# Block-diagonal operands of a block inverse: 48 small copies on one engine, or 16 wide copies on two

## The chip, the cores and the metric

The kernel runs on one core of a Trainium2 chip. The metric is the device time of one execution, in microseconds (us).

## The reference

One step of a diffusion backbone with one trunk layer, on 128 context tokens and 512 latent tokens of width 1024. A modulated RMSNorm is followed by one wide input projection. Its columns feed a bidirectional gated DeltaNet with 8 heads of size 128, a convolution branch and two merge gates; then come an output projection with a gated residual and a gated feed-forward part.

The change concerns the DeltaNet. For each head, direction and chunk of tokens a lower triangular system with unit diagonal is solved:

```
a_mat = where(strict, (k*beta) @ k.T * decay, 0) + I
sol   = triangular_solve(a_mat, [v*beta, k*beta*exp(gc)])
```

The kernel takes chunks of 128 tokens (five of them), and forms the inverse of the 128x128 matrix itself.

## The kernel before

The 640 tokens are the columns of all wide tiles. Heads are worked on in four pairs; a pair has 2 directions x 2 heads x 5 chunks = 20 matrices, ten for each direction. Every pair goes through the same stages, each a generator whose steps are interleaved by weights (`W_PREP`, `W_SUBST`, `W_BUILD`, `W_INV`, `W_SCAN`) with the projections of the later heads, the gates and the convolution (`mains`). What is written there is a program order with priorities; the order of each engine's queue is then settled at compile time from estimated costs. On the chip every engine works its queue in that order.

- `pair_prep` builds the 20 matrices `Bt` (VectorE and ScalarE, with a select on GpSimd, line 590), then inverts the 32x32 diagonal blocks of all of them at once by substitution: line 598 (ScalarE) and line 599 (VectorE) gather the blocks into `Cc`, line 601 transposes, line 604 masks, lines 610 and 612 are 30 steps of two small operations, on VectorE for three pairs and on GpSimd for the last (`SUBST_V`). Lines 616 and 617 write `T1` and `T2`: 32 partitions for each of four diagonal blocks, and for each partition 32 x 32 values, with the matrix number running innermost.
- `pair_inverse` spreads these blocks into block-diagonal 128x128 operands: `XA` from `T1` for the first direction and `T2` for the second, `XB` the other way round. This is line 631. A source element lies 128 bytes from the next. The operands are five tiles each of four matrices; four of the tiles hold four matrices of one direction, the fifth the last two of both. `XB` is cleared once at the start (line 447); `XA` in each pair (line 625), since its tiles are reused later for a product.
- `invert(k)` runs five lanes in turn, step by step: the off-diagonal part `ct` (GpSimd, line 654), products with `XA` (lines 665, 666), with `XB` (line 668), the square written back over `XA` (line 669), the rest (lines 671 to 680). All matmuls of these are in line 660.
- `pair_scan` and `pair_out` carry the state over the chunks and finish the heads.

Wherever a weight is loaded, ScalarE writes its high part (line 109) and VectorE or GpSimd its low part (line 110), before TensorE's projections in line 147. VectorE also runs the depthwise convolution of the other branch, one step for each tap (lines 847 to 854), with two inputs in SBUF. Line 873 evicts a projection through ScalarE, line 875 goes on with it on VectorE.

Of the kernel before, what the change touches and what calls it, by code (L numbers as in the profile page):

```python
# [11 lines left out]
F16 = mybir.dt.float16  # L12
BF16 = mybir.dt.bfloat16
I32 = mybir.dt.int32
AF = mybir.ActivationFunctionType
ALU = mybir.AluOpType
# [3 lines left out]
P = 128  # L20
# [25 lines left out]
W_BUILD = 2.0  # L46
# [12 lines left out]
def hybrid_step(ctx, tc, I, O):  # L59
    nc = tc.nc  # L60
    es = ctx.enter_context
    V, S_, G, PE = nc.vector, nc.scalar, nc.gpsimd, nc.tensor
# [11 lines left out]
    s1p = s1_open.enter_context(tc.tile_pool(name="s1", bufs=1))  # L74
# [10 lines left out]
    def const(name, shape, dt=F32, pool=None):  # L85
        return (pool or sb).tile(list(shape), dt, name=name, bufs=1)
# [18 lines left out]
    def bc(ap, shape):  # L105
        return ap.to_broadcast(shape)
# [66 lines left out]
    for k, (nm, n) in enumerate((("c_ctx", 8), ("c", 8), ("norm1", 8), ("norm2", 8))):  # L173
        src = I[nm] if nm == "c_ctx" else I[nm][0]
# [5 lines left out]
    ident = const("ident", [P, P])  # L180
# [51 lines left out]
    for n in range(2):  # L232
        for i in range(NCH):
            junk = T_("C", "junk")
            S_.activation(junk[:, :512], xs[n][:, i, :], AF.Square, accum_out=ss[:, i, n:n + 1])
            pt = sm_ps()
# [6 lines left out]
    for c0, cn in GRP:  # L243
        pt = g3(sm_ps(), 4)
# [19 lines left out]
    for pr in range(4):  # L264
# [7 lines left out]
        for kk in range(NK):  # L272
            for g in range(4):
                j, k = g // 2, g % 2
                PE.matmul(pa[32 * g:32 * g + 32, :P], sc[:, kk, 14:46], ws[j][:, kk, 128 * k:128 * k + 128],
                          start=(kk == 0), stop=(kk == NK - 1), tile_position=(0, 32 * g))
        br = T_("dd", "br")[:, :P]
        V.tensor_copy(br, pa[:, :P])
        pt = sm_ps()
        PE.transpose(pt[:, :P], br, ident)  # L280
        for k in range(2):
# [5 lines left out]
            for r, (c0, n) in enumerate(SPANS):  # L287
                v, hi, lo = (t[kt // 4][:, kt % 4, c0:c0 + n] for t in (xT, hh, hl))
                b = modB[:, kt, r:r + 1]
# [151 lines left out]

    y32s = [const("y32", [P, 512], pool=s1p)]
    L16 = [const(f"L16{i}", [P, 4, P], F16, s1p) for i in range(9)]
    XA = [const(f"XA{i}", [P, 4, P], F16, s1p) for i in range(5)]
    XB = [const(f"XB{i}", [P, 4, P], F16, s1p) for i in range(5)]
    for t in XB:
        G.memset(t, 0.0)

    def proj_in(col, after=None):
        w = pre.pop(col, None) or load_w(cols_of(w_in, col), after=after)  # L450
# [169 lines left out]

    def pair_inverse(R):
        Bt, Bn, T1, T2 = R.Bt, R.Bn, R.T1, R.T2
        groups = [((0, 4, k % 2, 4 * (k // 2)),) for k in range(4)] + [((0, 2, 0, 8), (2, 2, 1, 8))]
        for k, parts in enumerate(groups):
            G.memset(XA[k], 0.0)
            for o, cnt, d, n0 in parts:
                n0 += 10 * d
                for b in range(4):
                    r = slice(32 * b, 32 * b + 32)
                    for dst, src in ((XA[k], T1 if d == 0 else T2), (XB[k], T2 if d == 0 else T1)):  # L630
                        S_.activation(dst[r, o:o + cnt, 32 * b:32 * b + 32],  # L631
                                      src[r, :, n0:n0 + cnt].rearrange("p o n -> p n o"), AF.Identity)
            yield W_BUILD
        Bd = Bt[:, :2560].rearrange("p (d n i) -> p d n i", d=2, n=10)

        def invert(k):
            xa, xb = XA[k], XB[k]
            ct, a, atr = L16[3 * k:3 * k + 3]
            zt, a2, yt, rr = ct, xa, atr, a
            if k < 4:  # L640
                d, n0 = k % 2, 4 * (k // 2)
                B4, off = Bd[:, d, n0:n0 + 4, :], off16[:, d:d + 1, :]
                shape = [P, 4, P]

                def v(t):
                    return t
            else:
                B4, off = Bd[:, :, 8:10, :], off16.unsqueeze(2)
                shape = [P, 2, 2, P]

                def v(t):
                    return t.rearrange("p (a b) i -> p a b i", a=2)
            blocks = [B4[:, j, :] if k < 4 else B4[:, j // 2, j % 2, :] for j in range(4)]
            G.tensor_tensor(out=v(ct), in0=B4, in1=bc(off, shape), op=ALU.mult)
            yield

            def mm4(lhs, rhs):
                pt = g3(sm_ps(), 4)
                for j in range(4):
                    PE.matmul(pt[:, j, :], lhs[j], rhs[:, j, :], start=True, stop=True)  # L660
                return pt

            def l4(t):
                return [t[:, j, :] for j in range(4)]
            S_.activation(a, mm4(l4(ct), xa), AF.Identity)
            S_.activation(atr, mm4(l4(xa), ct), AF.Identity)
            yield
            V.tensor_tensor(out=zt, in0=mm4(l4(a), xb), in1=xb, op=ALU.add)
            S_.activation(a2, mm4(l4(atr), a), AF.Identity)
            yield  # L670
            V.tensor_tensor(out=yt, in0=mm4(l4(a2), zt), in1=zt, op=ALU.add)
            yield
            ptr = g3(sm_ps(F16), 4)
            for j in range(4):
                PE.transpose(ptr[:, j, :], yt[:, j, :], ident16)
            y32 = g3(y32s[k % 2], 4)
            S_.activation(y32, ptr, AF.Identity)
            V.tensor_tensor(out=rr, in0=mm4(blocks, y32), in1=bc(ident.unsqueeze(1), [P, 4, P]), op=ALU.add)
            yield
            V.tensor_tensor(out=B4, in0=v(mm4(l4(rr), yt)), in1=v(yt), op=ALU.add)  # L680
            yield

        lanes = [invert(k) for k in range(5)]
        while lanes:
            for ln in list(lanes):
                if next(ln, 0) == 0:
                    lanes.remove(ln)
                else:
                    yield W_INV
        R.Y1 = Bn  # L690
# [596 lines left out]
```

## Time and profile before

| | |
|---|---|
| median of 3 runs | 1381.05 us (1378.54 to 1384.46) |
| the profiled execution | 1383.22 us, its span 1381.2 us |
| TensorE busy | 1291.9 us, 94% of the span |
| VectorE busy | 839.1 us, 61% |
| ScalarE busy | 542.0 us, 39% |
| GpSimd busy | 306.8 us, 22% |
| mean granted clock of TensorE | 0.973 of full speed |

In the profile PE is TensorE, DVE is VectorE, ACT is ScalarE, POOL is GpSimd; L631 is line 631 of the kernel. Matmuls are pipelined and their ends are modelled, so a busy TensorE is not one at its peak. A row of a timeline merges neighbouring instructions of one kind (x6 for six), gives their start and length, and in brackets how long the engine stood idle before them and what it was then released by. A row of stretches gives from:to and length, then the busy time (and instructions) of PE, of its weight loads, of DVE, ACT and POOL, or of the one engine concerned, and last TensorE's granted clock, the busy share of the DMA engines and GB/s.

### The profile page before, as it was taken

The page shows a single profiled execution, that of the slowest core. Times are in us where ns is not written, and L with a number is a line of the kernel's source. Part 1 is how long each engine was busy: PE and PEld are TensorE (multiplying, and loading weights), DVE is VectorE, ACT ScalarE, POOL GpSimd, SP SyncE. Part 2 cuts the span into 40 slices and gives each one's busy share as a digit, 9 for nine tenths or more (in the row PEclk, how much of TensorE's full clock was granted, in tenths as well). Part 3 has the DMA queues.
Part 4 walks back from the last instruction along what each step waited for, and adds up shares of the span by engine and source line. Part 5 has one row for each costly group of instructions (what it writes and reads, how often), then busy time and mean ns, then how long its engine had stood idle before and what let it go on. Part 6 is the DMA issues. An engine that isn't in the chain of part 4 may idle for free.

```text
span 1381.2 us, 23408 instructions
## 1 busy us (share of the span) xinstructions
PE 1291.9 (94%) x9180; PEld 1213.3 (88%) x9180; DVE 839.1 (61%) x1603; ACT 542.0 (39%) x1240; POOL 306.8 (22%) x354
## 2 busy tenths in 40 slices
PE   4998996978999998988999989999999999999997
PEld 4998895977998998888989988889998999989996
DVE  5788985978667899596577774731223321233236
ACT  3337647263454555526454133332221222212223
POOL 2103310200010310291010025433310333003314
PEclk8999998999999999998999999999999999999999
DMA  9523442343343543323346884122222222222222
GB/s 289 140 64 113 125 149 80 112 136 100 113 119 99 160 118 94 103 66 94 118 150 212 250 284 148 46 74 77 77 77 76 77 77 77 76 76 69 71 77 91
DMA packets 180334, 157.31 MB, mean 114 GB/s; under 512 B 9072, under 2 KB 151809, under 8 KB 180225
## 3 DMA queue, kind: packets, MB, share of 16 engines
q1 hardware_dynamic: 180225, 155.83, 36.5%
q8 instruction: 72, 1.18, 0.4%
q14 instruction: 37, 0.30, 0.1%
HBM read 131.80 MB, written 24.00 MB: 113 GB/s over the span
## 4 chain that ended last, share of the span: by engine, by line
PE 68%; DVE 13%; ACT 6%; DMA 5%; issue 4%; POOL 1%; SPq 1%; POOLq 0%; DVEq 0%; ACTq 0%
PE mm L147 46%; PE sm L1115 9%; PE mm L1115 4%; DMA wr<-in_w_in 3%; ACT XA L631 2%; ACT XB L631 2%; PE sm L660 2%; DVE wl L110 1%; DVE uacc L847 1%; DVE acc L484 1%; PE sm L736 1%; ACT wh L109 1%; PE sm L495 1%; PE mm L469 1%; DMA og<-ogd 1%
## 5 line engine op out<-in xcount | busy, mean ns | idle before, releaser
L109 ACT ACTIVATE wh<-wr 128x1024 fp32r<-128x1024 f32 (+1 forms) x154 | 152.6, 992 | 497.5 <-PE mm L147 209.3
L147 PE MATMUL mm<-hh,wh 128*128 128x256 f32 (+1 forms) x896 | 219.7, 320 | 11.6 <-ACT wh L109 7.8
L147 PE MATMUL mm<-hl,wh 128*128 128x256 f32 (+1 forms) x896 | 218.0, 317 | 0.0
L147 PE MATMUL mm<-hh,wl 128*128 128x256 f32 (+1 forms) x896 | 216.4, 317 | 0.0
L110 POOL TENSOR_TENSOR wl<-wr,wh 128x1024 fp32r<-128x1024 f32 (+1 forms) x59 | 133.2, 2260 | 345.9 <-ACT wh L109 337.5
L110 DVE TENSOR_TENSOR wl<-wr,wh 128x1024 fp32r<-128x1024 f32 (+1 forms) x95 | 110.0, 1158 | 126.0 <-ACT wh L109 114.9
L147 PEld LDWEIGHTS mm<-hh,wh 128*128 128x128 f32 x896 | 163.5, 192 | 17.7 <-ACT wh L109 8.3
L147 PE MATMUL mm<-h2h,wh 128*128 128x256 f32 (+1 forms) x704 | 165.0, 312 | 1.5 <-ACT h2h L109 1.5
L147 PEld LDWEIGHTS mm<-hl,wh 128*128 128x128 f32 x896 | 166.3, 192 | 0.0
L147 PE MATMUL mm<-h2l,wh 128*128 128x256 f32 (+1 forms) x704 | 164.9, 312 | 0.9 <-POOL h2l L110 0.9
L147 PEld LDWEIGHTS mm<-hh,wl 128*128 128x128 f32 x896 | 164.6, 191 | 0.5 <-DVE wl L110 0.2
L147 PE MATMUL mm<-h2h,wl 128*128 128x256 f32 (+1 forms) x704 | 164.3, 311 | 0.3 <-DVE wl L110 0.3
L1253 DVE TENSOR_TENSOR ft<-ft,mm 128x384 f32<-128x384 f32 (+1 forms) x44 | 19.7, 484 | 198.8 <-PE mm L147 198.6
L147 PEld LDWEIGHTS mm<-h2l,wh 128*128 128x128 f32 x704 | 130.5, 191 | 1.1 <-POOL h2l L110 1.1
L147 PEld LDWEIGHTS mm<-h2h,wh 128*128 128x128 f32 x704 | 129.2, 190 | 1.9 <-ACT h2h L109 1.7
L147 PEld LDWEIGHTS mm<-h2h,wl 128*128 128x128 f32 x704 | 130.0, 190 | 0.6 <-DVE wl L110 0.6
L484 DVE SCALAR_TENSOR_TENSOR acc<-ci,colA,acc 128x642 f32<-128x642 f32 x96 | 85.9, 895 | 7.8 <-ACT acc L482 7.2
L1115 PE MATMUL sm<-wh,fl 128*128 128x512 f32 x152 | 60.0, 395 | 0.0
L1115 PE MATMUL sm<-wh,fh 128*128 128x512 f32 x152 | 59.9, 394 | 0.0
L1115 PE MATMUL sm<-wl,fh 128*128 128x512 f32 x152 | 59.7, 392 | 0.0
L110 DVE TENSOR_TENSOR fl<-ft,fh 128x640 fp32r<-128x640 f32 x22 | 47.7, 2167 | 15.5 <-ACT fh L109 15.5
L847 DVE SCALAR_TENSOR_TENSOR uacc<-u,colB,uacc 128x113 f32<-128x113 f32 (+14 forms) x120 | 47.8, 399 | 0.9
(341 smaller groups left out, 2431.7 us busy)
## 6 DMA issues: line engine op xcount, KB each, us to landing
wr<-in_w_in SPq DMA_DIRECT2D x56, 512.0 KB
wr<-in_w_gu SPq DMA_DIRECT2D x44, 512.0 KB
wr<-in_w_ada SPq DMA_DIRECT2D x32, 512.0 KB
wr<-in_w_down SPq DMA_DIRECT2D x22, 512.0 KB
wada<-in_w_ada SPq DMA_DIRECT2D x8, 1024.0 KB
atd<-et SPq DMA_DIRECT2D x40, 128.0 KB
aux<-atd SPq DMA_DIRECT2D x40, 128.0 KB
tgd<-tgt SPq DMA_DIRECT2D x16, 320.0 KB
```

What stands on the lines that cost most here:

```text
L109: S_.activation(hi, x, AF.Identity)
L110: return (lo_eng or V).tensor_tensor(out=lo, in0=x, in1=hi.bitcast(F32), op=ALU.subtract)
L147: PE.matmul(out, a[:, kt, :], x, start=(kt == 0 and j == 0), stop=(kt == nk - 1 and j == 2))
L469: PE.matmul(pa[32 * g:32 * g + 32, :], sc[:, kt, o:o + 32], w[:, c:c + P], start=(bb == 0), stop=(bb == 1), tile_position=(0, 32 * g))
L484: V.scalar_tensor_tensor(out=acc[:, :n], in0=ci[:, k:k + n], scalar=vA[:, k, ct:ct + 1], in1=acc[:, :n], op0=ALU.mult, op1=ALU.add)
L495: PE.transpose(pt[:, c, :], src(c0 + c), ident)
L631: S_.activation(dst[r, o:o + cnt, 32 * b:32 * b + 32], src[r, :, n0:n0 + cnt].rearrange("p o n -> p n o"), AF.Identity)
L660: PE.matmul(pt[:, j, :], lhs[j], rhs[:, j, :], start=True, stop=True)
L736: PE.matmul(pv[:, d, j, :], Y1[:, d, j, ck[d], :], rhs, start=True, stop=True)
L847: V.scalar_tensor_tensor(out=acc[:, a0:128 - a1], in0=u[:, a0 + dl:128 - a1 + dl], scalar=tap(k, t4), in1=acc[:, a0:128 - a1], op0=ALU.mul ...
L1115: PE.matmul(acc[i], a[kt // 4][:, kt % 4, c], b[:, k2, :], start=(kt == 0 and j == 0), stop=(kt == nk - 1 and j == 2))
L1253: V.tensor_tensor(out=d, in0=d, in1=s, op=ALU.mult)
```

## The change

The ten tiles become two, `XA` and `XB`, each with all 20 matrices of a pair. One copy now moves the same diagonal block of all ten matrices of a direction: 8 copies on ScalarE for `XA`, 8 on GpSimd for `XB`, in place of 48 on ScalarE. `XA` is cleared by one write in place of five, `XB` too. The lanes read and write slices of the two tiles; the operations on them keep their engines and sizes. The fill yields twice with 2.5 times the weight instead of five times.

```diff
--- before.py
+++ after.py
@@ -441,10 +441,8 @@
 
     y32s = [const("y32", [P, 512], pool=s1p)]
     L16 = [const(f"L16{i}", [P, 4, P], F16, s1p) for i in range(9)]
-    XA = [const(f"XA{i}", [P, 4, P], F16, s1p) for i in range(5)]
-    XB = [const(f"XB{i}", [P, 4, P], F16, s1p) for i in range(5)]
-    for t in XB:
-        G.memset(t, 0.0)
+    XA, XB = (const(nm, [P, 2, 10, P], F16, s1p) for nm in ("XA", "XB"))
+    G.memset(XB.rearrange("p d n i -> p (d n i)"), 0.0)
 
     def proj_in(col, after=None):
         w = pre.pop(col, None) or load_w(cols_of(w_in, col), after=after)
@@ -620,64 +618,63 @@
 
     def pair_inverse(R):
         Bt, Bn, T1, T2 = R.Bt, R.Bn, R.T1, R.T2
-        groups = [((0, 4, k % 2, 4 * (k // 2)),) for k in range(4)] + [((0, 2, 0, 8), (2, 2, 1, 8))]
-        for k, parts in enumerate(groups):
-            G.memset(XA[k], 0.0)
-            for o, cnt, d, n0 in parts:
-                n0 += 10 * d
-                for b in range(4):
-                    r = slice(32 * b, 32 * b + 32)
-                    for dst, src in ((XA[k], T1 if d == 0 else T2), (XB[k], T2 if d == 0 else T1)):
-                        S_.activation(dst[r, o:o + cnt, 32 * b:32 * b + 32],
-                                      src[r, :, n0:n0 + cnt].rearrange("p o n -> p n o"), AF.Identity)
-            yield W_BUILD
+        G.memset(XA.rearrange("p d n i -> p (d n i)"), 0.0)
+        for d in range(2):
+            for b in range(4):
+                r = slice(32 * b, 32 * b + 32)
+                S_.activation(XA[r, d, :, 32 * b:32 * b + 32],
+                              (T1, T2)[d][r, :, 10 * d:10 * d + 10].rearrange("p o n -> p n o"), AF.Identity)
+                G.tensor_copy(XB[r, d, :, 32 * b:32 * b + 32],
+                              (T2, T1)[d][r, :, 10 * d:10 * d + 10].rearrange("p o n -> p n o"))
+            yield 2.5 * W_BUILD
         Bd = Bt[:, :2560].rearrange("p (d n i) -> p d n i", d=2, n=10)
 
         def invert(k):
-            xa, xb = XA[k], XB[k]
             ct, a, atr = L16[3 * k:3 * k + 3]
-            zt, a2, yt, rr = ct, xa, atr, a
+            zt, yt, rr = ct, atr, a
             if k < 4:
                 d, n0 = k % 2, 4 * (k // 2)
                 B4, off = Bd[:, d, n0:n0 + 4, :], off16[:, d:d + 1, :]
+                xa, xb = XA[:, d, n0:n0 + 4, :], XB[:, d, n0:n0 + 4, :]
                 shape = [P, 4, P]
 
                 def v(t):
                     return t
             else:
                 B4, off = Bd[:, :, 8:10, :], off16.unsqueeze(2)
+                xa, xb = XA[:, :, 8:10, :], XB[:, :, 8:10, :]
                 shape = [P, 2, 2, P]
 
                 def v(t):
                     return t.rearrange("p (a b) i -> p a b i", a=2)
-            blocks = [B4[:, j, :] if k < 4 else B4[:, j // 2, j % 2, :] for j in range(4)]
+
+            def l4(t):
+                return [t[:, j, :] if len(t.shape) == 3 else t[:, j // 2, j % 2, :] for j in range(4)]
+            a2 = xa
             G.tensor_tensor(out=v(ct), in0=B4, in1=bc(off, shape), op=ALU.mult)
             yield
 
             def mm4(lhs, rhs):
                 pt = g3(sm_ps(), 4)
                 for j in range(4):
-                    PE.matmul(pt[:, j, :], lhs[j], rhs[:, j, :], start=True, stop=True)
+                    PE.matmul(pt[:, j, :], lhs[j], rhs[j], start=True, stop=True)
                 return pt
-
-            def l4(t):
-                return [t[:, j, :] for j in range(4)]
-            S_.activation(a, mm4(l4(ct), xa), AF.Identity)
-            S_.activation(atr, mm4(l4(xa), ct), AF.Identity)
+            S_.activation(a, mm4(l4(ct), l4(xa)), AF.Identity)
+            S_.activation(atr, mm4(l4(xa), l4(ct)), AF.Identity)
             yield
-            V.tensor_tensor(out=zt, in0=mm4(l4(a), xb), in1=xb, op=ALU.add)
-            S_.activation(a2, mm4(l4(atr), a), AF.Identity)
+            V.tensor_tensor(out=v(zt), in0=v(mm4(l4(a), l4(xb))), in1=xb, op=ALU.add)
+            S_.activation(a2, v(mm4(l4(atr), l4(a))), AF.Identity)
             yield
-            V.tensor_tensor(out=yt, in0=mm4(l4(a2), zt), in1=zt, op=ALU.add)
+            V.tensor_tensor(out=yt, in0=mm4(l4(a2), l4(zt)), in1=zt, op=ALU.add)
             yield
             ptr = g3(sm_ps(F16), 4)
             for j in range(4):
                 PE.transpose(ptr[:, j, :], yt[:, j, :], ident16)
             y32 = g3(y32s[k % 2], 4)
             S_.activation(y32, ptr, AF.Identity)
-            V.tensor_tensor(out=rr, in0=mm4(blocks, y32), in1=bc(ident.unsqueeze(1), [P, 4, P]), op=ALU.add)
+            V.tensor_tensor(out=rr, in0=mm4(l4(B4), l4(y32)), in1=bc(ident.unsqueeze(1), [P, 4, P]), op=ALU.add)
             yield
-            V.tensor_tensor(out=B4, in0=v(mm4(l4(rr), yt)), in1=v(yt), op=ALU.add)
+            V.tensor_tensor(out=B4, in0=v(mm4(l4(rr), l4(yt))), in1=v(yt), op=ALU.add)
             yield
 
         lanes = [invert(k) for k in range(5)]
```

## Rows read from the trace of the kernel before

**Rows 1.** Stretches of the span: from:to, length, busy us of each engine.

```profile
120.00:200.00 80.00, 77.80 (x642) 71.89 (x641) 72.98 (x145) 47.07 (x145) 25.96 (x35) 1.00 0.42 132
...
300.00:400.00 100.00, 93.74 (x824) 87.56 (x823) 79.42 (x177) 46.24 (x117) 7.90 (x23) 1.00 0.36 110
```

**Rows 2.** The chain of waits, shares by line.

```profile
by line: PE mm L147 45.5%; PE sm L1115 8.9%; PE mm L1115 4.2%; issue 3.8%; DMA wr<-in_w_in 2.6%; ACT XA L631 2.1%; ACT XB L631 1.8%; PE sm L660 1.6%; DVE wl L110 1.3%; DVE uacc L847 1.2%; DVE acc L484 1.0%; PE sm L736 1.0%; ACT wh L109 0.9%
```

**Rows 3.** Timeline of ScalarE behind the first fill: start, length.

```profile
223.82 0.60 ACT L665 ACTIVATE L<-sm 128x512 f16<-128x512 f32 x1
...
224.93 1.90 ACT L598 ACTIVATE Cc<-Bt 32x320 f32<-32x320 f32 x4
...
227.65 1.06 ACT L109 ACTIVATE wh<-wr 128x1024 fp32r<-128x1024 f32 x1
```

**Rows 4.** Line 631 alone in the four stretches where it runs.

```profile
208.16:223.80 15.64, 15.41 (x48) 0.93 0.35 106
...
275.78:291.62 15.84, 15.60 (x48) 0.95 0.29 88
...
538.57:554.46 15.89, 15.64 (x48) 0.95 0.26 67
...
634.86:651.72 16.86, 15.82 (x48) 0.90 0.28 82
```

**Rows 5.** Timeline of TensorE where it stood idle.

```profile
209.92 0.38 PE L660 MATMUL sm<-XA,L 128*128 128x128 f16 x4 [1.46 <-ACT XA L631]
...
220.36 0.38 PE L660 MATMUL sm<-XA,L 128*128 128x128 f16 x4 [3.75 <-ACT XA L631]
...
224.47 0.59 PE L660 MATMUL sm<-XA,L 128*128 128x128 f16 x4 [2.94 <-ACT L L665]
...
229.33 0.55 PE L147 MATMUL mm<-hh,wh 128*128 128x256 f32 x1 [3.78 <-DVE tz L875]
...
292.73 0.90 PE L147 MATMUL mm<-hh,wh 128*128 128x256 f32 x2 [7.08 <-ACT wh L109]
...
555.10 0.59 PE L566 MATMUL sm<-maskadd,ident_b 128*128 128x512 bf16 x1 [6.54 <-ACT K L540]
...
649.48 2.08 PE L736 MATMUL sm<-r,Bt 128*128 128x128 f32 x8 [3.41 <-ACT Sn L749]
```

**Rows 6.** Stretches behind TensorE's stops, first of four, and their sum.

```profile
224.47:235.26 10.79, 7.01 (x35) 6.19 (x34) 8.12 (x16) 8.65 (x17) 1.26 (x1) 0.50 0.18 66
...
sum 25.17, PE 21.38 PEld 19.73 DVE 17.82 ACT 19.27 POOL 1.26; mean PE 5.35 PEld 4.93 DVE 4.46 ACT 4.82 POOL 0.32
```

**Rows 7.** The stretches of the first two fills that hold stops.

```profile
208.10:229.40 21.30, 9.36 (x81) 8.24 (x79) 6.20 (x11) 20.88 (x60) 0.87 (x2) 0.82 0.29 91
284.90:292.80 7.90, 0.82 (x18) 0.47 (x17) 1.28 (x4) 7.78 (x26) 0.00 (x0) 0.82 0.06 8
```

**Rows 8.** Groups of ScalarE by shape, 200 to 720: busy us, mean ns.

```profile
L631 ACT ACTIVATE XA<-T 32x128 f16<-32x128 f32 x64 | 26.1, 425 | 9.7 <-DVE T L616 9.1
...
L631 ACT ACTIVATE XA<-T 32x64 f16<-32x64 f32 x32 | 9.7, 302 | 0.2
...
L598 ACT ACTIVATE Cc<-Bt 32x320 f32<-32x320 f32 x12 | 5.6, 467 | 1.1 <-POOL Bt L590 1.0
```

**Rows 9.** Groups of GpSimd by shape, whole span.

```profile
L590 POOL TENSOR_SCALAR_AFFINE_SELECT Bt<-Bt 128x640 f32<-128x640 f32 x16 | 14.7, 942 | 95.4 <-DVE Bt L584 95.4
...
L612 POOL TENSOR_TENSOR X<-X,stmp 128x240 f32<-128x240 f32 x2 | 1.3, 671 | 0.2
```

**Rows 10.** Timeline of GpSimd in the last pair's substitution.

```profile
622.33 1.49 POOL L612 TENSOR_TENSOR X<-X,stmp 128x130 f32<-128x130 f32 x1
```

**Rows 11.** Timeline of VectorE ahead of the second substitution.

```profile
209.29 2.05 DVE L599 STREAM_TRANSPOSE Cc<-Bt 32x320 f32<-32x320 f32 x4
```

**Rows 12.** Line 847, 584 to 622 and 640 to 690: ns min/median/max.

```profile
L847 DVE SCALAR_TENSOR_TENSOR uacc<-u,colB,uacc x30: 321/608/772, 585.1 to 621.9; 128x113 f32<-128x113 f32 x2, 128x114 f32<-128x114 f32 x2, 128x115 f32<-128x115 f32 x2, 128x116 f32<-128x116 f32 x2
...
L847 DVE SCALAR_TENSOR_TENSOR uacc<-u,colB,uacc x30: 330/342/357, 640.6 to 672.0; 128x113 f32<-128x113 f32 x2, 128x114 f32<-128x114 f32 x2, 128x115 f32<-128x115 f32 x2, 128x116 f32<-128x116 f32 x2
```

## The prediction

> **What bounds the kernel now.** I read the busy shares in stretches first, then the chain of waits by line, then the timelines of ScalarE and TensorE around the four places where the operands of the inverse are filled, one per pair of heads. In the stretch that holds the pairs TensorE is the engine that is nearly always at work (93.7 of 100 us from 300 to 400 us) and VectorE comes next (79.4; 73.0 of 80 from 120 to 200) [rows 1]. ScalarE is busy about half the time and bounds nothing on average. Yet the chain of waits holds 2.1% + 1.8% of the span, 3.9% of 1381.2 = 53.9 us, on ScalarE at line 631, the small copies [rows 2].
>
> The reason is their shape in time. The 48 copies of a pair run back to back, for 15.64, 15.84, 15.89 and 16.86 us [rows 4], and ScalarE works in order: what stands behind them (the evictions of lines 665 and 666, the copies of line 598 that start the next pair's substitution, the weight splits of line 109, the evictions of projections) waits for the whole block [rows 3]. TensorE lives on what it already has, then stops: 1.46 + 3.75 + 2.94 + 3.78 = 11.93 us in the first pair, then 7.08, 6.54 and 3.41 us [rows 5], 28.96 us in all, each put down to ScalarE, or to a VectorE step behind a ScalarE one. After each stop the granted clock is 0.50 for a while, the lower of the two levels (1.2 of 2.4 GHz): 21.38 us of TensorE's work fall in these four stretches [rows 6], half of which, 10.7 us, is lost. Together 28.96 + 10.7 = 39.7 us hang on the blocks. In the longest stop VectorE works 1.28 of 7.90 us and the DMA engines 6% [rows 7]: neither is what TensorE waits for.
>
> **The change, part by part.**
>
> *Removed on ScalarE:* 48 copies per pair, 32 of 128 elements per partition (425 ns) and 16 of 64 (302 ns) [rows 8]; the block is some 15.8 us with overlaps.
>
> *Added on ScalarE:* 8 copies of 320 elements per partition. No row shows one with this read pattern (each element 128 bytes from the last). Below: a copy of 320 elements on 32 partitions with rows of 32 in place takes 0.467 us (line 598). Above: in the old shapes' own pace, 320/128 of 425 ns, 1.06 us. From the two old shapes a further element costs (425 - 302)/64 = 1.92 ns, so 302 + 256 x 1.92 = 794 ns [rows 8]; neighbours overlap a little, so I take 0.75 us. The block becomes 8 x 0.75 = 6.0 us (3.7 to 8.5), 9.8 us less per pair.
>
> *Moved to GpSimd:* 8 copies per pair, beside ScalarE's. Nearest rows: a select with one tensor input takes 942 ns for 640 elements, so 0.47 for 320 if all of it scales; an add with two inputs takes 671 ns for 240, so 0.89 for 320 [rows 9]; and one add of 130 elements that ran beside a VectorE split took 1.49 us [rows 10]. With one input but a spread read I take 0.7 us: 8 x 0.7 = 5.6 us, bounds 3.8 and 11.9. GpSimd is idle around the fills (0.87 us of work in the first 21 us) [rows 7], so little queues behind them: the select of line 604 for the next pair, which itself waits for the copies of line 598 on ScalarE. XB is first read at line 668, two stages after XA. The GPSIMD Engine Reference of the Trainium skill, under Performance pitfalls, says that a GpSimd read whose step exceeds 8 bytes costs about 2.9 cycles an element in place of 1.9; at its 1.2 GHz that would be an estimated 0.77 us a copy and 6.2 us a pair, still beside ScalarE's 6.0, and no run here shows it yet.
>
> *What covers the new block.* From a block's start to the point where TensorE runs out there are 9.9 us in pair 1 (292.73 - 7.08 - 275.78), 10.0 in pair 2 and 11.2 in pair 3 [rows 4, 5]. A block of 6.0 us plus the weight split behind it (1.06 us, line 109) [rows 3] ends inside that, so these three stops go, and with them their slow clock. In the first pair TensorE reaches XA 1.46 us before the first four small copies are done; it now needs the four wide ones of that direction, 3.0 us, so this stop grows to 2.7 us, and the others go: eight wide copies end 6.0 us after the start, against 8.45 when TensorE next stops (220.36 - 3.75 - 208.16) [rows 4, 5]. What is left of 39.7 us is 2.7; gain 37.0.
>
> *The two tiles in place of ten.* A lane waits for the part that it reads, if waits follow parts of a tile. They do here: VectorE wrote its half of Cc at 209.29 us, while ScalarE wrote the other half, ahead of it in the program, only at 224.93 [rows 3, 11]. The clearing of XA becomes one write of five times the size; it must follow the last lane of the pair before, not its own lane. For pair 0 nothing is ahead, for the others the old lanes end long before the next block. I cost it and the unchanged sizes of the inverse's own steps at nothing; if that cover fails it is a few us a pair.
>
> *VectorE beside GpSimd.* Thirty of the depthwise-conv taps with two SBUF inputs have a median of 0.608 us while GpSimd runs the last pair's substitution, and thirty of the same sizes 0.342 us with GpSimd idle [rows 12]. SBUF — State Buffer, of the Trainium skill, under Who interferes with whom, says that a VectorE instruction with two SBUF inputs and a GpSimd one that reads SBUF block each other for the whole instruction; the trace agrees in kind, with 0.27 us a tap. During 5.6 us of GpSimd copies VectorE loses at most 5.6 x (1 - 0.342/0.608) = 2.5 us a pair, 10 in all; it is often in other work there, so I take 3 us.
>
> **The sum.** Two ledgers. TensorE's stops and clock: 37.0 us. The chain: its 53.9 us on the copies become 4 x 6.0 = 24.0, so 29.9 us. The second is lower because other waits stand close behind, so I take it, less 3 us for VectorE: 27 us. The profiled execution took 1383.2 us, of which the span is 1381.2; it becomes 1356. The median of the runs shown is 2.2 us below the profiled one, so I forecast 1354 us.
>
> Bounds of this case: with 0.467 us a copy the chain keeps 15 us, so 39 us go, and all of 39.7 is the most that the blocks hold: 1341. With 1.06 us a copy the chain keeps 34 us, so 20 go, less the 10 of VectorE: 1371.
>
> **Rivals.**
>
> 1. *The next wait takes a good part.* VectorE is busy 91% of the time in some stretches [rows 1], and its own chains (substitution, taps) may end just behind ScalarE's. For it: the first pair's last stop of 3.78 us already names VectorE [rows 5]. Against it: VectorE too stood still in the stops, so it moves up as well [rows 7]. If half of 29.9 us comes back as other stops: 1381 - 15 + 3 = 1369.
>
> 2. *The order.* Each engine's order is fixed at compile time from estimated costs, and new costs give a new order of all the work around. An order in which a needed VectorE step stands behind a run of taps costs stops as large as those removed (3.78 us in the first pair is put down to one) [rows 5]. If eight to ten new ones of 3 to 4 us appear, the gain is gone: 1381, 1374 to 1390. This is also the case where the change does what it says on ScalarE and nothing reaches the end. For it: the order does move; against it: the removed stops were all of one cause.
>
> 3. *Slower: GpSimd and VectorE block each other.* Place: the eight copies of each pair. If each takes 1.49 us [rows 10] and VectorE stands still for all of it, VectorE loses 11.9 us a pair, 48 in all, against 37 gained: 1381 + 11 = 1392. It counts as slower from a loss of about 44 us, 11 us a pair or 1.4 us a copy. Against it: the taps lost 0.27 us each [rows 12], and much of VectorE's work around the fills has one SBUF input. The rule of SBUF — State Buffer (the Trainium skill), above, would bring this about if VectorE always came second with an instruction of that kind.
>
> **How the numbers follow.** About 0.5% (6.9 us) is what a measurement of this kernel can tell from no change, so faster means below 1374 and slower above 1388. Forecast (1341 to 1367, since both upper bounds at once are unlikely; near 1354): 0.54. Rival 1 (1367 to 1374): 0.23. Rival 2: 0.15, of which 0.10 within 0.5% and 0.05 slower. Rival 3: 0.08, slower. Faster 0.77, same 0.10, slower 0.13. The forecast and rival 1 together are 0.77; a range of 1341 to 1379 takes in a part of rival 2 and leaves out about 0.2. The likeliest case's own range is 1341 to 1367.
>
> **What the profile after would show.** Four blocks of eight copies on ScalarE, about 6 us each, 0.75 us a copy; beside each, eight of 0.7 us on GpSimd, ending no later. The copies' share of the chain falls from 3.9% to under 1.8%. TensorE's stops of 7.08, 6.54 and 3.41 us and the slow clock behind them are gone; its idle time in the stretch of the pairs falls by some 25 us. VectorE's and GpSimd's instructions overlapping the copies are stretched by a quarter to a half microsecond, not more. The prediction is wrong if the copies are as forecast and stops of like size stand elsewhere (rivals 1 and 2), if TensorE waits for XB or GpSimd copies take over 1.2 us (rival 3), or if the wide ScalarE copies cost over 1 us.

## The result, and the profile after

The changed kernel takes 1357.42 us, the median of 4 executions (1356.62 to 1360.47), against 1382.35 for the kernel before beside it: a ratio of 0.9826, with a 95% interval of 0.9806 to 0.9846. The forecast was 1354, the gain forecast 27 us, the gain measured 24.9. The profiled execution has a span of 1354.9 us, 26.3 less than before, with a mean granted clock of 0.980 (0.973 before).

Line numbers are those of the changed kernel: 625 copies into `XA`, 627 into `XB`, 621 clears `XA`. Lines 675, 739, 844 and 847 are 678, 742, 847 and 850 of before. First the head of its page, with the busy time of each engine:

```profile
span 1354.9 us, 23233 instructions
...
PE 1282.6 (95%) x9180; PEld 1205.9 (89%) x9180; DVE 839.6 (62%) x1603; ACT 504.6 (37%) x1080; POOL 334.0 (25%) x366
```

TensorE does the same 9180 matmuls in 9.3 us less busy time (1291.9 before), and stands idle for 1354.9 - 1282.6 = 72.3 us, 17.0 less than before (1381.2 - 1291.9 = 89.3). Together these are the 26.3 us. Most of the 9.3 is slow clock gone: 49.3 us of TensorE's work ran at a granted clock of 0.50 before, 33.6 do now, and half of the difference is 7.9. The chain of waits could be followed back only to about 350 us, so its shares are not compared with [rows 2]; of the copies it holds two blocks, 7.7 us of GpSimd's in the third fill and 6.2 of ScalarE's in the last.

The copies, first one by one (tile `XA`, then tile `XB`: ns min/median/max, first and last start):

```profile
L625 ACT ACTIVATE XA<-T x32: 735/780/808, 208.1 to 612.6; 32x320 f16<-32x320 f32 x32
...
L627 POOL CAST XB<-T x32: 707/752/1674, 208.1 to 612.6; 32x320 f16<-32x320 f32 x32
```

Then as blocks, in the timeline of ScalarE and in that of GpSimd (start, length):

```profile
208.11 3.05 ACT L625 ACTIVATE XA<-T 32x320 f16<-32x320 f32 x4 [3.58 <-DVE T L614]
211.59 3.06 ACT L625 ACTIVATE XA<-T 32x320 f16<-32x320 f32 x4
...
273.87 6.36 ACT L625 ACTIVATE XA<-T 32x320 f16<-32x320 f32 x8 [2.02 <-DVE T L614]
...
607.05 6.30 ACT L625 ACTIVATE XA<-T 32x320 f16<-32x320 f32 x8 [2.80 <-DVE T L614]
```

```profile
208.14 6.12 POOL L627 CAST XB<-T 32x320 f16<-32x320 f32 x8 [5.91 <-DVE T L614]
...
273.90 6.94 POOL L627 CAST XB<-T 32x320 f16<-32x320 f32 x8 [9.25 <-DVE T L614]
...
522.41 8.03 POOL L627 CAST XB<-T 32x320 f16<-32x320 f32 x8 [8.21 <-DVE T L614]
...
607.09 6.29 POOL L627 CAST XB<-T 32x320 f16<-32x320 f32 x8 [4.37 <-DVE T L614]
```

ScalarE's blocks of 15.64 to 16.86 us [rows 4] are now 6.30 to 6.95 us (the third runs from 523.70 to 530.65, with a step between its halves). GpSimd's run beside them. What this does to TensorE is seen in the stretches of the four fills:

```profile
208.10:214.80 6.70, 3.24 (x21) 2.81 (x20) 3.81 (x7) 6.55 (x10) 6.24 (x9) 0.73 0.23 86
273.80:280.90 7.10, 7.10 (x68) 6.71 (x66) 5.29 (x11) 6.91 (x10) 6.62 (x8) 1.00 0.68 218
522.40:530.70 8.30, 8.30 (x64) 8.19 (x63) 8.30 (x8) 8.08 (x12) 7.93 (x9) 1.00 0.34 103
607.00:613.50 6.50, 6.50 (x54) 6.48 (x52) 2.27 (x6) 6.34 (x9) 5.97 (x8) 1.00 0.31 97
```

In the last three fills TensorE is busy in every microsecond, at a granted clock of 1.00; before, it stopped for 7.08, 6.54 and 3.41 us behind them [rows 5] and then ran at 0.50 [rows 6]. In the first it still waits. Its timeline, where it stood idle for longest:

```profile
211.21 0.58 PE L660 MATMUL sm<-XA,L 128*128 128x128 f16 x4 [2.16 <-ACT XA L625]
...
214.70 0.58 PE L660 MATMUL sm<-XA,L 128*128 128x128 f16 x4 [1.31 <-ACT XA L625]
...
304.99 0.71 PE L743 MATMUL sm<-vw,K 128*128 128x128 f32 x4 [2.51 <-DVE vw L739]
...
591.46 0.91 PE L660 MATMUL sm<-L,L 128*128 128x128 f16 x7 [6.21 <-DVE aux L675]
...
780.76 2.39 PE L792 MATMUL sm<-ident,oacc 128*128 128x128 f32 x10 [2.93 <-DVE oacc L780]
```

Counting every stop of 0.4 us or more from 205 to 860 us, before has 50.0 us, of which 29.0 at the fills [rows 5]; after has 33.9, of which 2.16 + 1.31 = 3.5 at the fills. So 25.5 us left the fills and 9.4 us came back elsewhere: between 680 and 790 us (700 to 815 before) stops grew from 6.8 to 12.5 us, and in the second pair's scan (285 to 318 us after, two stops of 1.2 us before) from 2.4 to 5.9. The 6.21 us stop is hardly new: with one of 1.64 before it, it stands where before had 2.00, 3.50 and two small ones, 6.7 in all.

The gain doesn't arise pair by pair. The second fill starts 1.9 us earlier than before (273.87 against 275.78), the third 14.9 (523.70 against 538.57), the last 27.8 (607.05 against 634.86). TensorE's idle time from 260 to 340 us fell only from 11.9 to 9.1 us, although its largest stop there was removed.

### The profile page after: what moved, and what is told of

It reads as the page before. It is cut to its first block, busy times and chain, and to the rows that moved or that the text cites. A ratio compares the mean times of both kernels' runs of the same rounds, so it can differ in the third digit from the quotient of the medians.

```text
span 1354.9 us, 23233 instructions
## 1 busy us (share of the span) xinstructions
PE 1282.6 (95%) x9180; PEld 1205.9 (89%) x9180; DVE 839.6 (62%) x1603; ACT 504.6 (37%) x1080; POOL 334.0 (25%) x366
## 4 chain that ended last, share of the span: by engine, by line
PE 58%; DVE 6%; issue 3%; ACT 2%; DMA 2%; POOL 2%; POOLq 0%; SPq 0%; DVEq 0%; ACTq 0%
PE mm L147 38%; PE sm L1112 9%; PE mm L1112 4%; PE sm L660 1%; DVE uacc L844 1%; PE sm L733 1%; DMA mad<-te 1%; PE sm L713 1%; DVE uacc L851 1%; PE sm L720 1%; PE sm L743 1%; PE sm L757 1%; PE sm L1157 1%; DMA og<-ogd 1%; POOL XB L627 1%
## 5 line engine op out<-in xcount | busy, mean ns | idle before, releaser
L147 PE MATMUL mm<-hh,wl 128*128 128x256 f32 (+1 forms) x896 | 212.9, 314 | 0.0
L844 DVE SCALAR_TENSOR_TENSOR uacc<-u,colB,uacc 128x113 f32<-128x113 f32 (+14 forms) x120 | 51.1, 426 | 0.8
```

What stands on the lines that cost most here:

```text
L147: PE.matmul(out, a[:, kt, :], x, start=(kt == 0 and j == 0), stop=(kt == nk - 1 and j == 2))
L844: V.scalar_tensor_tensor(out=acc[:, a0:128 - a1], in0=u[:, a0 + dl:128 - a1 + dl], scalar=tap(k, t4), in1=acc[:, a0:128 - a1], op0=ALU.mul ...
```

## The experiments

Each kernel was timed beside the kernel before on the same chip (medians 1382.35 to 1383.16); the ratios are to that. Three questions were open: whether the width of the copies, the sharing between engines or the two tiles made the gain; whether GpSimd beside VectorE costs anything; and how far the order alone moves the time.

**Which part of the change does it.** All sixteen wide copies on ScalarE (e1; here and below an edit is shortened at `...`):

```diff
-                G.tensor_copy(XB[r, d, :, 32 * b:32 * b + 32],
-                              (T2, T1)[d][...].rearrange("p o n -> p n o"))
+                S_.activation(XB[r, d, :, 32 * b:32 * b + 32],
+                              (T2, T1)[d][...].rearrange("p o n -> p n o"), AF.Identity)
```

> All 16 wide copies of a pair on ScalarE, in the same two tiles. Block theory (what counts is how long ScalarE's block holds the work behind it, against some 10 us that TensorE has in hand): 16 x 0.78 us = 12.5 us a block, 2.5 to 4 us too long in pairs 1 to 3 and some 5 us in the first pair, so stops of about 14 us and some 5 us of slow clock come back on the 1357 us of the changed kernel: 1370 to 1376 us. Rival, tiles and order (the two tiles and the new order of the work around bring the gain, not the length of the block): about 1357 us. Rival, number of copies (each instruction on ScalarE costs, the length does not): 16 for 48, about 1361 us.

It took 1377.93 us, 0.9974 (0.9958 to 0.9989), above the 1370 to 1376 expected. ScalarE's timeline at the first fill, and then two of TensorE's stops:

```profile
207.95 3.11 ACT L625 ACTIVATE XA<-T 32x320 f16<-32x320 f32 x4 [3.56 <-DVE T L614]
211.09 3.16 ACT L627 ACTIVATE XB<-T 32x320 f16<-32x320 f32 x4
...
214.69 3.04 ACT L627 ACTIVATE XB<-T 32x320 f16<-32x320 f32 x4
217.74 2.97 ACT L625 ACTIVATE XA<-T 32x320 f16<-32x320 f32 x4
```

```profile
220.76 0.58 PE L660 MATMUL sm<-XA,L 128*128 128x128 f16 x4 [4.44 <-ACT XA L625]
...
544.69 0.58 PE L564 MATMUL sm<-maskadd,ident_b 128*128 128x512 bf16 x1 [3.64 <-ACT L L662]
```

This block is 12.8 us long, the others 13.2 to 14.3, and the second half of `XA` comes last in it: TensorE waits for that, and elsewhere for what stands behind the block. Sixteen wide copies on one engine are worth 0.3% of the whole time. Up to the last fill they are worth more: it starts at 618.8 us, 16.0 earlier than in the kernel before, where the changed kernel's starts 27.8 earlier. Behind it 12 us are lost again, a good part in two stretches at a clock of 0.50 (731 to 742 and 796 to 813 us, 8.3 and 11.1 us of TensorE's work). So the small total is not the price of the blocks alone; why the rest is slower here was not pursued.

The kernel before, with its ten tiles and 48 small copies, 24 of a pair on GpSimd (e2):

```diff
-                    for dst, src in ((XA[k], ...), (XB[k], ...)):
-                        S_.activation(dst[r, o:o + cnt, ...], src[...], AF.Identity)
+                    S_.activation(XA[k][r, o:o + cnt, ...], (T1, T2)[d][...], AF.Identity)
+                    G.tensor_copy(XB[k][r, o:o + cnt, ...], (T2, T1)[d][...])
```

> The kernel before with its ten tiles and small copies, the 24 copies of XB of a pair on GpSimd. Block theory: ScalarE's block is 24 copies, about 8 us, inside the 10 us that TensorE has in hand; GpSimd's 24 copies of 0.3 to 0.45 us take about 9.5 us beside it; the four stops go and the time is 1357 to 1364 us. Rival, width (the wide shape brings the gain): little or half of it, 1369 us or more. Rival, tiles and order: 1382 us, as before.

1356.5 us, 0.9811 (0.9786 to 0.9836): all of the gain, without a single wide copy. GpSimd's first block:

```profile
208.77 8.93 POOL L632 CAST XB<-T 32x128 f16<-32x128 f32 x24 [6.01 <-DVE T L616]
```

ScalarE's blocks are 9.1 to 9.7 us here, GpSimd's 8.9 to 12.7. At the first fill stops of 2.20 us (for `XA`) and 1.25 us are left, behind the third one of 1.32; no matmul waits for work behind the second. The blocks lie just inside the 9.9 to 11.2 us of cover which the prediction read; e1's lie outside.

The two tiles, with 48 small copies on ScalarE as before (e4; the lines taken out are those of the changed kernel's copies):

```diff
...
+                for n0, cnt in ((0, 4), (4, 4), (8, 2)):
+                    for dst, src in ((XA, (T1, T2)[d]), (XB, (T2, T1)[d])):
+                        S_.activation(dst[r, d, n0:n0 + cnt, ...], src[r, :, 10 * d + n0:...], AF.Identity)
```

> The two tiles and one clearing of the changed kernel, filled by 48 small copies of a pair on ScalarE (4, 4 and 2 matrices a copy). Block theory: the block is 15 to 16 us as before and the time 1378 to 1386 us. Rival, tiles and order: the gain of the changed kernel is there without its copies, 1357 to 1365 us. If it lies well above 1386 us, the order that the tiles bring costs time by itself, and the copies' gain is larger than the result shows.

1376.55 us, 0.996 (0.9944 to 0.9977). The stops of the fills are still there (5.50 us at the first, 7.42 at the second, 5.71 at the third). The tiles alone are worth about 0.4%; where that comes from was not pursued. Width alone gives 0.3% of the time (e1), and nothing more once the copies are shared (e2): what brings the whole gain is that half the block leaves ScalarE.

**Any third place.** `XB`'s copies on VectorE instead of GpSimd (e6: `G.tensor_copy` becomes `V.tensor_copy`):

> The changed kernel with the eight copies of XB on VectorE in place of GpSimd. VectorE theory (VectorE has no room where the fills are, so the copies belong on the idle engine): eight copies of some 0.45 us, 3.6 us a pair and 14 us in all, delay its splits and the substitution; 1362 to 1372 us. Rival, any third place will do (it is enough that ScalarE's block is 6 us): 1354 to 1360 us.

1355.53 us, 0.9784 (0.9753 to 0.9816), not to be told from the changed kernel. Its tile view of `XB`:

```profile
L627 DVE CAST XB<-T x32: 382/441/522, 208.9 to 607.0; 32x320 f16<-32x320 f32 x32
```

Eight copies are 3.5 us of VectorE's time a pair, which it had to spare here.

**GpSimd made to hurt.** All sixteen on GpSimd (e3: `S_.activation` of `XA` becomes `G.tensor_copy`):

> All 16 wide copies of a pair on GpSimd, none on ScalarE. Block theory: ScalarE holds nothing up; GpSimd's block is 16 x 0.78 us = 12.5 us, and the first lane gets XA after 6 to 7 us in place of 3; TensorE waits some 3 us more at its first product with XA where that product stands early in its order: 1355 to 1366 us. Rival, GpSimd and VectorE block each other: twice the GpSimd work beside VectorE costs at least what the first half did; the time is above 1370 us. Rival, two engines are needed because the sum of the copies is what sets the path: 12.5 us in a row on any engine costs as much as on ScalarE, 1370 to 1376 us.

1384.01 us, 1.0019 (1.0005 to 1.0034). The second fill in GpSimd's timeline, and TensorE's there:

```profile
301.91 3.26 POOL L625 CAST XA<-T 32x320 f16<-32x320 f32 x4 [8.01 <-DVE T L614]
305.23 7.05 POOL L627 CAST XB<-T 32x320 f16<-32x320 f32 x8
312.34 2.96 POOL L625 CAST XA<-T 32x320 f16<-32x320 f32 x4
```

```profile
305.22 0.58 PE L660 MATMUL sm<-XA,L 128*128 128x128 f16 x4 [10.85 <-POOL XA L625]
...
315.35 0.58 PE L660 MATMUL sm<-XA,L 128*128 128x128 f16 x4 [9.12 <-POOL XA L625]
```

This looks like GpSimd as the bound, and the second stop is that: `XA`'s second half stands behind `XB`. But the first is not. The fill begins at 301.9 us instead of 273.9, and VectorE's timeline of this kernel shows why:

```profile
299.00 0.20 DVE L610 TENSOR_TENSOR X<-X,stmp 128x30 f32<-128x30 f32 x1
299.10 0.35 DVE L844 SCALAR_TENSOR_TENSOR uacc<-u,colB,uacc 128x118 f32<-128x118 f32 x1
299.36 0.67 DVE L847 SCALAR_TENSOR_TENSOR uacc<-u,colB,uacc 128x432 f32<-128x432 f32 x1
299.93 1.91 DVE L614 STREAM_TRANSPOSE T<-X 128x1024 f32<-128x1024 f32 x1
```

Among the steps of the pair's substitution (lines 608 and 610) stand taps of the convolution: 50 of them, 26 us, between the first fill and the transpose into `T` (line 614), where the changed kernel has one. So that transpose starts at 299.9 us; in the changed kernel at 271.8. GpSimd worked 0.15 us from 280 to 300 us, so it didn't stretch these: the order did.

Each of GpSimd's copies made twice, `XA` on ScalarE (e5: `for _ in range(2): G.tensor_copy(...)`), to see when GpSimd is late:

> The changed kernel with each copy of XB done twice on GpSimd: 16 wide copies there, 12.5 us, ScalarE's block as changed. Cover theory (XB is first read two stages after XA, so GpSimd's half has several us to spare and VectorE loses little): 1355 to 1364 us. Rival, GpSimd and VectorE block each other or GpSimd's half is as long as the path allows: each further us of GpSimd work costs about one, 6.2 us a pair, so 1370 to 1382 us.

1374.79 us, 0.9948 (0.993 to 0.9966). The number alone would fit a GpSimd that is late. TensorE's longest stop says otherwise:

```profile
308.26 0.59 PE L661 MATMUL sm<-XA,L 128*128 128x128 f16 x4 [9.96 <-ACT XA L625]
```

It waits for ScalarE's `XA`; again the second fill slid, to 305.1 us, with VectorE busy for 20.00 of the 20 us ahead of 300. That is one stop from the order; what blocks of 14 to 16 us on GpSimd cost the kernel by themselves can't be read here, because the order moved with them.

**Which delay counts: `XA`'s, or that of the work behind the block.** Three kernels copy all of `XA` ahead of `XB`, with each engine's copies held in that order, and differ in the engines: both share each operand (e9, whose edit is shown), all on GpSimd (e10), all on ScalarE (e11); in the last two the choice by `b` is gone.

```diff
+        for X_, Ts in ((XA, (T1, T2)), (XB, (T2, T1))):
+            for d in range(2):
+                for b in range(4):
...
+                    if b < 2:
+                        ins, e = S_.activation(dst, src, AF.Identity), 0
+                    else:
+                        ins, e = G.tensor_copy(dst, src), 1
+                    if e in last:
+                        order(ins, last[e])
```

> The same 16 wide copies, eight an engine as in the changed kernel, but each operand is shared: two of four diagonal blocks on ScalarE, two on GpSimd, XA of both directions first and XB behind it on either engine, in that order. ScalarE's block stays 6.3 us; XA of a direction is there after 1.6 and 3.1 us in place of 3.1 and 6.5. Latency theory (TensorE's remaining waits for XA, 2.16 and 1.31 us in the first pair of the changed kernel, hang on when XA lands): 2 to 5 us below the changed kernel, 1352 to 1356 us. Block theory (only the length of ScalarE's block counts): 1357 us, within 3. Rival, order: the new order of the work around gives anything within 6 us of it.

> All 16 wide copies on GpSimd, with XA of both directions first and XB behind it; in the run with all on GpSimd the order was XA, XB, XB, XA, and TensorE stood 10.9 and 9.1 us in the second pair for the two halves of XA. Latency theory (that run lost its gain because the second half of XA stood behind all of XB): the second stop falls from 9.1 to some 3 us, the other copies are off ScalarE: 1357 to 1368 us. Rival, total length on one engine: 12.5 us of copies in a row cost the same in any order, 1378 to 1386 us.

> All 16 wide copies on ScalarE, XA of both directions first and XB behind it; in the run with all on ScalarE the order was XA, XB, XB, XA. Latency theory (what counts is when XA of the second direction lands, 6.3 us here and 12.4 there, against 15 in the kernel before): most of the gain is there, 1357 to 1366 us. Block theory (what stands behind the 12.5 us on ScalarE, the weight splits and the evictions of the first products, is late as in that run): 1372 to 1380 us.

e9: 1356.64 us, 0.9818 (0.9798 to 0.9838), no gain over the changed kernel. `XA` is early and the two stops for it are gone, but at 219.18 us TensorE stands 4.94 us for the eviction of the inverse's first product: ScalarE comes to it (at 218.55) only behind its block, four copies into `Cc` and a weight split. e10: 1381.69 us, 0.9988 (0.9972 to 1.0005), where 1357 to 1368 was expected; it lies in the rival's 1378 to 1386. The second stop for `XA` fell from 9.12 to 2.62 us, as it should; the first stayed (10.26), with the fill at 298.95 us. e11: 1379.86 us, 0.9982 (0.9965 to 0.9999). From TensorE's timeline of e11:

```profile
224.96 0.39 PE L147 MATMUL mm<-hh,wh 128*128 128x256 f32 x1 [3.58 <-ACT wh L109]
...
287.73 0.90 PE L147 MATMUL mm<-hh,wh 128*128 128x256 f32 x2 [5.09 <-ACT wh L109]
```

`XA` was there after its first eight copies, and still TensorE stood, for weights which ScalarE writes behind the block. That is the prediction's step: the length of ScalarE's block is what costs, more than when `XA` is complete. As in e1 the total hides a part: in the profiled execution e11's last fill starts 6.7 us earlier than in the kernel before, and 8 us are lost behind it.

**The order alone.** `W_BUILD`, the weight of the stage with the fill, 4.0 in place of 2.0, in the changed kernel (e12) and in the kernel before (e13):

```diff
-W_BUILD = 2.0
+W_BUILD = 4.0
```

> The changed kernel with the interleaving weight of the fill doubled (4 in place of 2): the same instructions on the same engines, only the program order around the fills, and with it each engine's order, is another. Copies theory (the two short blocks bring the gain in any reasonable order): 1350 to 1364 us. Rival, order (the gain needs the order that this kernel happened to get): it moves by more than 7 us, to 1364 us or more.

> The kernel before with the same weight doubled: the same instructions, another order. Copies theory: the 16 us blocks on ScalarE cost as much in any order, 1374 to 1390 us. Rival, order: a kernel with 48 small copies on ScalarE comes below 1370 us by order alone.

e12: 1361.09 us, 0.9832 (0.9809 to 0.9856): the gain holds in another order. e13: 1396.06 us, 1.0086 (1.0057 to 1.0114), outside of what either theory expected: the same work of before, ordered otherwise, costs 13 us more. Its longest stop is 8.00 us at 653.80, put down to the scan's `vw` on VectorE. One step further back it is ScalarE's block again, which runs from 639.32 to 656.56 us: VectorE had waited 6.23 us for `vn`, an eviction that ScalarE makes 13.4 us into its copies (VectorE's row, then ScalarE's):

```profile
653.32 0.76 DVE L742 TENSOR_TENSOR vw<-sm,dec 128x256 f32<-128x256 f32 x2 [6.23 <-ACT vn L738]
```

```profile
652.69 0.60 ACT L738 ACTIVATE vn<-sm 128x512 f32<-128x512 f32 x1
```

So a weight can move a kernel by half of what this change brought, and the order decides how much the blocks cost: with the weight at 4.0 the change is worth 35 us (1396.06 to 1361.09), with 2.0 it is worth 25.

**The longest stop that is left.** The last pair's substitution on VectorE, as for the other three, instead of GpSimd, in the changed kernel (e7):

```diff
-SUBST_V = (1, 1, 1, 0)
+SUBST_V = (1, 1, 1, 1)
```

> The changed kernel with the last pair's substitution on VectorE too, as for the first three pairs. In the changed kernel TensorE stands 1.64 and 6.21 us behind VectorE while GpSimd runs that substitution and the conv taps take 0.64 us in place of 0.34. Contention theory (these stops come from GpSimd's two-input steps stretching the taps): they go, and with the slow clock behind them 8 to 10 us, less what 60 more steps (some 20 us) on VectorE cost in a stretch where it is full: 1350 to 1360 us. Rival, VectorE is full: the time rises, 1362 us or more.

1342.69 us (1341.78 to 1344.76), 0.9703 (0.968 to 0.9726): the best version, 14.7 us below the changed kernel by the medians. Line 844 from 555 to 625 us, first in the changed kernel, then in e7 (ns min/median/max):

```profile
L844 DVE SCALAR_TENSOR_TENSOR uacc<-u,colB,uacc x30: 324/606/1243, 566.5 to 601.5; 128x113 f32<-128x113 f32 x2, 128x114 f32<-128x114 f32 x2, 128x115 f32<-128x115 f32 x2, 128x116 f32<-128x116 f32 x2
```

```profile
L844 DVE SCALAR_TENSOR_TENSOR uacc<-u,colB,uacc x35: 325/335/342, 572.5 to 624.9; 128x113 f32<-128x113 f32 x3, 128x114 f32<-128x114 f32 x3, 128x115 f32<-128x115 f32 x3, 128x116 f32<-128x116 f32 x3
```

VectorE's timeline of the changed kernel shows how the 6.21 us stop came about:

```profile
584.08 0.68 DVE L675 TENSOR_TENSOR L<-sm,ident 128x512 f16<-128x512 f32 x1
584.68 0.47 DVE L851 SCALAR_TENSOR_TENSOR uacc<-u,colB,uacc 128x256 f32<-128x256 f32 x1
...
585.77 0.83 DVE L851 SCALAR_TENSOR_TENSOR uacc<-u,colB,uacc 128x192 f32<-128x192 f32 x1
...
589.18 1.62 DVE L844 SCALAR_TENSOR_TENSOR uacc<-u,colB,uacc 128x127 f32<-128x127 f32 x3
590.73 0.68 DVE L675 TENSOR_TENSOR aux<-sm,ident 128x512 f16<-128x512 f32 x1
```

Between two steps of the inverse that TensorE waits for stand 6 us of taps, all but the first of them stretched beside GpSimd's steps with two inputs. In e7 the taps are back at 335 ns and the stop is 0.65 us:

```profile
586.33 0.38 PE L660 MATMUL sm<-L,L 128*128 128x128 f16 x4 [0.65 <-DVE aux L675]
```

From 570 to 660 us TensorE's idle time falls from 8.1 to 1.1 us, and the granted clock rises from 0.94 to 1.00. Later, from 680 to 860 us, idle time falls from 12.8 to 8.5. e7 moved the order too, so how much is the stretch and how much the order is not separated.

## Why the prediction was right

- **What binds.** ScalarE's blocks held TensorE, through the work queued behind them. Shown: halving the block by wide copies (this change), by small ones (e2) or with VectorE's help (e6) gives the same time; blocks of 12.6 to 14.3 us of wide copies on ScalarE alone (e1, e11) give almost nothing in the end, whichever operand comes first, though 12 and 8 us of that are lost behind the last fill; and in e11 TensorE stood for weights behind the block when `XA` was long complete. Not shown is that emptying ScalarE altogether is worth as much: in e3 and e10 the order moved as well.
- **The copies.** ScalarE's took 0.78 us (0.75 forecast, from the slope of the two old shapes), its blocks 6.3 to 7.0 (6.0). GpSimd's took 0.75 in the median (0.7), its blocks 6.1 to 8.0 (5.6). It ended later than ScalarE in the second fill by 0.6 us, where "no later" was forecast, and no matmul waited for it. (`XB` is read one step of a lane behind `XA`, not two; TensorE first reads it at 225.0 us, 10.7 behind the end of GpSimd's first block.) The GPSIMD Engine Reference of the Trainium skill, under Performance pitfalls, has the 2.9 cycles an element from which the prediction estimated 0.77 us for this spread read; the trace agrees, with 0.752.
- **The cover.** Forecast 9.9 to 11.2 us; the stops at the second, third and last fill were gone at blocks of up to 9.7 us (e2, but for 1.32 us). Behind the longer blocks of e1 and e11 stops of 3.6 to 5.1 us stood at the first and third fill, and at the second in e11; but at the second in e1 only 1.07, and behind the last ones, of 14.2 us, nothing above 0.6. So the cover is no fixed length: it moves with the order. The first pair's was to grow to 2.7 us and be the only one; it became 2.16 + 1.31 = 3.5, since the second four copies were waited for as well.
- **Slow clock.** 10.7 us were forecast to go with the stops. At the fills TensorE's work at 0.50 fell from 21.38 us [rows 6] to 5.38, which gives back 8.0: the first pair's two stops are still followed by slow clock, which the ledger had left out. Elsewhere among the pairs and behind them such work grew by some 10 us, the most at 777.7, and costs 5. And a stretch of 6.24 us at 914.7, far behind the last pair, was gone: another 3.1. (The rest of the 7.9 us lies in the first 115 us, where it bought no time: the first fill starts at 208.1 us as before.) First the stretch at 914.7 in the kernel before, then two in the changed kernel:

```profile
914.70:921.50 6.80, 6.24 (x29) 6.24 (x30) 0.00 (x0) 0.15 (x1) 1.74 (x2) 0.50 0.00 0
```

```profile
211.10:217.90 6.80, 5.38 (x29) 5.12 (x29) 1.44 (x4) 6.61 (x12) 3.41 (x6) 0.50 0.00 0
...
777.70:791.40 13.70, 8.32 (x32) 7.40 (x32) 8.61 (x16) 2.22 (x3) 2.12 (x2) 0.50 0.67 217
```

- **The sum.** TensorE's ledger said 37.0, the chain 29.9, and the lower one, less 3 us, was taken. What left the fills is 25.5 us of stops and 8.0 of slow clock, 33.5. What came back elsewhere is 9.4 us of stops and 5 of slow clock, about 14, so rival 1 (the next wait) was real at nearly the 15 us of its price. That leaves some 19 us of the 26.3. Another 3.1 are the slow clock at 914.7, which no part of the prediction explains; the last 4 are idle times below 0.4 us and busy time that these rows don't account for. So the mechanism is right, and that the number came out within 3 us is in part luck. TensorE's idle time fell by 17.0 us, where some 25 were to show.
- **VectorE beside GpSimd.** At most 2.5 us a pair were forecast. In the third fill it was more: six taps took 0.4 to 0.5 us longer each and a weight split 0.6, together 3.6 us (against the medians of the same shapes where GpSimd is idle; rows below). The second fill cost 0.8 us, the first and last nothing, since VectorE had no taps there: 4.4 us in all, near the 3 that were taken. One GpSimd copy of 32 took 1.67 us, above the 1.2 that was named as a sign of rival 3, but no matmul waited for `XB`: rival 3 is refuted at this dose. At twice the dose (e3, e5) VectorE's instructions were stretched by some 16 us, counted the same way; what that costs the kernel at a fixed order stays open, since in e3, e5 and e10 the order of VectorE's work changed as well.
- **The order.** Rival 2 did not decide here, but it is of the size that the prediction feared: 13 us in e13 (there partly through ScalarE's block), and a second fill 25 to 31 us later in e3, e5 and e10.
- **Not foreseen.** The change needs neither wide copies nor two tiles (e2). And the second pair hardly moved up: its fill waits for VectorE's substitution, whose steps began 7.6 us earlier (224.5 against 232.1) but took 44.7 us in place of 41.3; the gain is collected at the third and fourth.

## What to carry to other kernels

A block of small instructions on an engine that is 39% busy can still bound the kernel: compare its length with what the busiest engine has in hand when it starts, and bring it under that, by sharing it with whatever engine is free, before making its instructions larger. After a change read again who fills the time between two steps of a chain that the busiest engine waits for: the largest gain that was left here (e7) was one such place. An experiment that changes costs changes a planned order as well, so a time that fits a theory proves little until the stops name that theory's engine (e5), and a stop has to be followed back further than the first engine named (e13).

## What the runs showed of the hardware

The same spread read, 320 elements on 32 partitions from f32 to f16, takes 0.78 us on ScalarE, 0.75 on GpSimd and 0.44 on VectorE; ScalarE's copy of 320 elements with rows in place, f32 to f32, took 0.467 [rows 8].

GpSimd's copies have one input, and they stretch VectorE's taps with two all the same. VectorE's timeline in the changed kernel, where GpSimd's block ends at 530.44 us:

```profile
525.26 1.79 DVE L110 TENSOR_TENSOR wl<-wr,wh 128x1024 fp32r<-128x1024 f32 x1
...
528.94 0.84 DVE L844 SCALAR_TENSOR_TENSOR uacc<-u,colB,uacc 128x127 f32<-128x127 f32 x1
529.71 1.27 DVE L847 SCALAR_TENSOR_TENSOR uacc<-u,colB,uacc 128x504 f32<-128x504 f32 x1
530.89 0.34 DVE L844 SCALAR_TENSOR_TENSOR uacc<-u,colB,uacc 128x126 f32<-128x126 f32 x1
531.15 0.73 DVE L847 SCALAR_TENSOR_TENSOR uacc<-u,colB,uacc 128x496 f32<-128x496 f32 x1
```

A tap of 127 elements takes 0.84 us beside a copy, one of 126 elements 0.34 behind the last of them; one of 504 takes 1.27, one of 496 0.73. Each loses about half a microsecond at either size; the weight split takes 1.79 us where 1.23 is the median with GpSimd idle. GpSimd's block is longer as well (8.03 us against 6.12 in the first fill). SBUF — State Buffer, of the Trainium skill, under Who interferes with whom, has the two block each other for a whole instruction; the trace agrees in kind, with 0.5 us a tap where a copy takes 0.75.
